# Gate and up products of both feed-forwards by Strassen's seven quarter products, the down products in a phase of their own

## The chip, the cores and the metric

The kernel runs on one core of one Trainium2 chip. The metric is the device time of one execution in microseconds (us). TensorE (PE) does the matrix products, VectorE (DVE), ScalarE (ACT) and GpSimd (POOL) the elementwise work, and every transfer between the chip's memory (DRAM) and SBUF is issued by SyncE's queue (SP). Each engine takes its own instructions in their written order.

## The reference

A network of two blocks over 1024 tokens with 1024 features. The first block holds two feed-forwards with a mixer between them:

```python
def swiglu(h, w_gu, w_down):
    g, u = jnp.split(h @ w_gu, 2, axis=-1)
    return (jax.nn.silu(g) * u) @ w_down
...
mod = (cs @ w_ada[l] + b_ada[l]).reshape(B, N_MOD, D)[:, :, None, :]
sh1, sc1, gt1, sh2, sc2, gt2, sh3, sc3, gt3 = [mod[:, i] for i in range(N_MOD)]
h = modulate(rms_norm(x, g_ffn1[l]), sh1, sc1)
x = x + HALF_STEP * gt1 * swiglu(h, w_gu1[l], w_down1[l])
h = modulate(rms_norm(x, g_mix[l]), sh2, sc2)
x = x + gt2 * hybrid_mixer(h, w_in[l], gate_bias[l], g_q[l], g_k[l], g_mh[l], w_out[l])
h = modulate(rms_norm(x, g_ffn2[l]), sh3, sc3)
x = x + HALF_STEP * gt3 * swiglu(h, w_gu2[l], w_down2[l])
```

`w_gu` is 1024 x 5632 (gate columns, then up columns), `w_down` 2816 x 1024. The mixer and the second block (two layers of attention, convolution and Fourier mixing) stand outside the change. Everything is float32.

## The kernel before

The program holds activations with the features on partitions: `H[k][h]` is feature block k (128 rows, k = 0..7) of token half h (512 columns). A float32 product is done as three products of rounded parts: each operand is split into a high part, rounded by ACT, and a low part, the remainder by DVE (`split`), and `gemm` issues high·high, high·low and low·high for each k, three matmuls of 128x128 by 128x512 (L311, L312, L313).

The 2816 hidden features of a feed-forward are 22 blocks of 128. `ffn` runs `gu(f, h)` for each block f and half h: 8 k x 3 matmuls for gate, as many for up, then `swiglu`: silu on ACT (L245), the product with up on DVE (L536), the split of the result (L250 on ACT, L272 on DVE) into the pair `act[f, h]`. A whole block is 96 matmuls. The blocks stand in groups of three (the last of four). After the first block of group g the down products of group g - 1 are issued, `out(g - 1, m, h)` for 8 output blocks m and both halves, each adding its result to the resident `X[m]` on DVE (L555). `Weights` loads each slab of weights and splits it ahead of its use.

Beside each block `fill(f)` starts one `ada` chunk, a piece of the modulation vector for later stages: four loads of 512 KB (`adaw`), eight multiply-adds into `adacc` on DVE (L437, L439), four transposes of `adacc` on PE (L452) and a sum on DVE (L454). `norm_mod` makes the second half of H (L490, L478) while the first blocks already run on half 0.

All tiles come from rotating pools: "u" with 43 tiles of 128x1024 (X, H, weights, act pairs, adaw), "hf" with 14 of 128x512 (e, adacc, sums), and eight PSUM banks (`ps`). A new tile waits for the last user of the buffer it takes. On SP each transfer also waits for the transfer eight earlier.

Of the kernel before, what the change touches and what calls it, by code (L numbers as in the profile page):

```python
# [18 lines left out]
P = 128  # L19
T = 1024  # L20
HT = 512
NK = 8
# [28 lines left out]
class Pipe:  # L51
    """Software pipeline over generators: each step moves every live one on to its next yield, oldest first.
    Streams set aside start their items beside whatever else is started."""
# [22 lines left out]

    def flush(self):
# [52 lines left out]
class Stream:  # L130
    """Items that are started at a rate."""
# [25 lines left out]
class Weights:  # L157
    """Slabs of weights, loaded and split ahead of their use."""

    def __init__(self, b, views, dve=False):  # L160
        self.b, self.views, self.dve = b, views, dve
        self.stg, self.w = [], []

    def fetch(self, n):
        while len(self.stg) < min(n, len(self.views)):
            self.stg.append(self.b.fetch_w(*self.views[len(self.stg)]))
# [12 lines left out]
    def get(self, i, ahead=1):  # L179
        """Slab i; the next ones are split, ahead of them, and the two behind these on their way."""  # L180
        self.split(i + 1)
        if ahead:
            self.fetch(i + 3 + ahead)
            self.split(i + 1 + ahead)
        return self.w[i]


class Build:
# [17 lines left out]
    # storage  # L206
# [4 lines left out]
    def pair(self, name="pair"):  # L211
        """High and low parts of a [128, 512] operand."""
# [14 lines left out]
    # activation tables  # L227
# [24 lines left out]
    def recip(self, out, in_):  # L252
        """out = 1 / in_ for in_ > 0."""
# [8 lines left out]
    def rsqrt(self, out, in_, scale, eps_col):  # L262
        """out = (in_ * scale + eps) ** -0.5"""
# [14 lines left out]
    def load(self, dst, src):  # L278
        """dst on chip <- src in DRAM (float32, rounded already where dst is float32r)."""
        self.nc.sync.dma_start(dst.bitcast(F32) if dst.dtype == F32R else dst, src)  # L280

    def store(self, dst, src):
        """dst in DRAM (float32) <- src on chip (float32 or rounded float32r)."""
        self.nc.sync.dma_start(dst, src.bitcast(F32) if src.dtype == F32R else src)

    # weights and products

    def fetch_w(self, view, kk, cc):
        s = self.U(F32, (P, kk, cc), "stg")
        self.load(s, view)  # L290
        return s
# [7 lines left out]
    def cols(self, w, starts):  # L299
        """Weights of the 128-column slabs of w (rows on partitions) that begin at starts."""  # L300
# [3 lines left out]
    def gemm(self, ps, w, col, H, h, parts=1, ks=None):  # L304
        """ps += W[:, col block].T @ H[:, half h]; w = (hi, lo) slabs, H[k][h] = (hi | lo) pairs. In parts."""
# [53 lines left out]
    def load_x(self, h):  # L359
        """Half h of X from tokens to features on partitions, and each token's 1 / rms on every partition."""  # L360
# [24 lines left out]
    def ada_start(self, w, c, bias, out, c0):  # L385
        """The same as ada, on the tensor engine."""
# [16 lines left out]
    def norm_start(self, X, r, a, s, H):  # L403
        """H[:][0] in two parts, each as soon as its modulation is there."""
# [14 lines left out]
    def ada(self, w, c, bias, out, c0, row=None, ahead=False):  # L419
        """out[:, c0/128 ...] = (c @ w)[c0 : c0 + 512] + bias, features on partitions;  # L420
        or 1 + that to DRAM, row = (where, bias)."""
# [10 lines left out]
        for q in range(4):  # L432
# [7 lines left out]
            if q % 2 and not ahead:  # L440
                yield
# [15 lines left out]
    # norms  # L457

    def add_sq(self, acc, x, first):
        """acc += x * x, for [128, 512] blocks."""  # L460
# [7 lines left out]
    def total(self, acc):  # L468
        """Sums over the partitions, on every partition."""
# [4 lines left out]
    def modulate(self, t, s, H, k, h):  # L474
        """H[k][h] = hi | lo of t + s."""
# [4 lines left out]
    def norm_mod(self, X, a, s, H, h, acc, r=None):  # L480
        """H[:][h] = X / rms(X) * a + s, acc = sums of squares or r = 1 / rms; a pipeline item."""
# [14 lines left out]
    # feed-forward  # L496

    def ffn(self, H, X, wgu, wdown, gate, fill, done, late, squares=True, begin=False):
# [5 lines left out]
        act, order, views = {}, {}, []  # L504

# [4 lines left out]
        def use_down(g):  # L510
            n = len(groups[g])
            for i in range(4):
                use(("down", g, i), wdown[i][:, groups[g][0]:groups[g][0] + n], n, 256)

        for g, grp in enumerate(groups):
            for f in grp:
                for o in range(2):
                    use((f, o), wgu[o * NFF + f], NK, P)
                if f == grp[0] and g:
                    use_down(g - 1)  # L520
        use_down(G - 1)
        ws = Weights(self, views)

# [8 lines left out]

        def swiglu(f, h, pg, pu):
# [4 lines left out]
            act[f, h] = p = self.pair("act")  # L538
            self.split(e, p[:, 0], p[:, 1])
# [8 lines left out]

        def out(g, m, h, acc=None):
            A = [[act[f, 0], act[f, 1]] for f in groups[g]]  # L550
            ps = self.ps()
            yield from self.gemm(ps, ws.get(order["down", g, m // 2]), (m % 2) * P, A, h)
# [11 lines left out]
        n = 2  # L564
        if begin:
            n = 3
# [10 lines left out]
        pipe.until(self.whole(H, 1))  # L577
        for f in range(n):
            pipe.go(gu(f, 1, 1 if f == n - 1 else 0))
        for f in range(n):  # L580
            fill(f)
# [1433 lines left out]
```

## Time and profile before

| | |
|---|---|
| time, median of 3 runs | 3357.47 us (3354.01 to 3358.36) |
| span of the profiled execution | 3352.6 us |
| PE busy | 3265.7 us, 97% |
| DVE, ACT, POOL busy | 59%, 38%, 6% |
| first feed-forward | about 33 to 760 us |
| second feed-forward | about 1490 to 2225 us |
| memory traffic | 368 MB, 110 GB/s over the span |

The profiled execution's own time is not listed apart from its span; the median of the runs lies 4.9 us above the span. PE's busy share is that of pipelined matmuls whose ends are modelled: the page gives one 128x512 matmul some 391 ns, while the next starts well before that, so what a matmul costs is read from the distance of starts in the timeline.

### The profile page before, as it was taken

How to read it: one execution, taken by the hardware profiler on the slowest of the kernel's cores; microseconds unless marked ns; L12 is line 12 of the kernel's file. 1: busy time of each engine (PE TensorE's matmuls, PEld its weight loads, DVE VectorE, ACT ScalarE, POOL GpSimd, SP SyncE). 2: the span in 40 equal slices, each digit the busy share in tenths (PEclk: the TensorE clock that was granted, in tenths of full speed). 3: DMA queues.
4: the chain of work that ended last, by engine and by line, in shares of the span. 5: the costliest groups of instructions: out<-in, count | busy, mean ns of one | idle time of the engine just before them, and what ended most of it. 6: DMA issues, size and time to landing. Idle time of an engine off the chain costs nothing.

```text
span 3352.6 us, 38177 instructions
## 1 busy us (share of the span) xinstructions
PE 3265.7 (97%) x14876; PEld 2673.0 (80%) x14876; DVE 1964.5 (59%) x2981; ACT 1263.3 (38%) x2063; POOL 198.2 (6%) x144
## 2 busy tenths in 40 slices
PE   8999999999999979999999999989999999999999
PEld 5888888887877768888888888878888777878877
DVE  7644543336378877666454332264746886565786
ACT  4111111124366554552111111244445834444770
POOL 0000000000122242410000000000000000000000
PEclk9999999999999979999999999999999999999999
DMA  5433321113444456453333211123421233332232
GB/s 209 151 121 113 118 90 52 55 57 113 147 139 134 120 166 183 123 196 120 113 114 110 63 48 47 60 88 118 121 81 58 89 138 127 119 111 64 73 135 107
DMA packets 131172, 368.05 MB, mean 110 GB/s; under 512 B 14872, under 2 KB 16792, under 8 KB 130992
## 3 DMA queue, kind: packets, MB, share of 16 engines
q1 hardware_dynamic: 130992, 365.62, 34.3%
q8 instruction: 117, 1.92, 0.2%
q14 instruction: 63, 0.52, 0.0%
HBM read 294.05 MB, written 71.51 MB: 109 GB/s over the span
## 4 chain that ended last, share of the span: by engine, by line
PE 87%; DVE 5%; ACT 4%; issue 2%; DMA 1%; POOL 0%; SPq 0%; DVEq 0%; ACTq 0%; POOLq 0%
PE ps L311 22%; PE ps L313 22%; PE ps L312 22%; PE ps L1431 2%; PE ps L1432 2%; PE ps L1433 2%; PE ps L1638 2%; PE ps L1714 1%; PE ps L1715 1%; PE ps L1713 1%; PE ps L1699 1%; PE ps L1700 1%; PE ps L619 1%; ACT bE L245 1%; DVE mS L276 1%
## 5 line engine op out<-in xcount | busy, mean ns | idle before, releaser
L311 PE MATMUL ps<-H,wh 128*128 128x512 f32 x2512 | 990.1, 394 | 15.9 <-ACT wh L250 12.1
L313 PE MATMUL ps<-H,wl 128*128 128x512 f32 x2512 | 982.8, 391 | 1.2 <-DVE wl L272 1.1
L312 PE MATMUL ps<-H,wh 128*128 128x512 f32 x2512 | 981.2, 391 | 0.0
L311 PEld LDWEIGHTS ps<-H,wh 128*128 128x128 f32 x2512 | 473.5, 189 | 119.2 <-ACT wh L250 13.3
L313 PEld LDWEIGHTS ps<-H,wl 128*128 128x128 f32 x2512 | 473.5, 189 | 103.3 <-DVE wl L272 3.0
L312 PEld LDWEIGHTS ps<-H,wh 128*128 128x128 f32 x2512 | 473.9, 189 | 98.8 <-issue 2.6
L272 DVE TENSOR_TENSOR wl<-stg,wh 128x1024 fp32r<-128x1024 f32 (+1 forms) x249 | 302.8, 1220 | 130.2 <-ACT wh L250 98.6
L250 ACT ACTIVATE wh<-stg 128x1024 fp32r<-128x1024 f32 (+1 forms) x233 | 232.4, 1009 | 310.5 <-PE ps L313 217.4
L536 DVE TENSOR_TENSOR e<-e,ps 128x512 f32<-128x512 f32 x88 | 60.5, 687 | 489.4 <-PE ps L313 489.3
L311 PE MATMUL ps<-act,wh 128*128 128x512 f32 x704 | 275.3, 391 | 0.0
L313 PE MATMUL ps<-act,wl 128*128 128x512 f32 x704 | 274.0, 389 | 0.0
L312 PE MATMUL ps<-act,wh 128*128 128x512 f32 x704 | 273.9, 389 | 0.0
L555 DVE SCALAR_TENSOR_TENSOR x<-ps,coef,x 128x512 f32<-128x512 f32 x224 | 167.5, 749 | 147.4 <-PE ps L313 147.3
L250 ACT ACTIVATE act<-e 128x512 fp32r<-128x512 f32 x88 | 55.6, 632 | 449.7 <-DVE e L536 443.3
L1641 DVE TENSOR_REDUCE bmc<-ps 128x1 f32<-128x512 f32 x256 | 164.6, 683 | 49.9 <-PE ps L1638 49.9
L245 ACT ACTIVATE e<-ps 128x512 f32<-128x512 f32 x88 | 52.5, 597 | 347.9 <-PE ps L313 347.9
L245 ACT ACTIVATE bE<-ps 128x512 f32<-128x512 f32 x256 | 138.2, 590 | 103.0 <-PE ps L1700 72.8
L276 DVE TENSOR_TENSOR bEl<-bE,bEh 128x1024 fp32r<-128x1024 f32 x128 | 155.2, 1218 | 33.4 <-ACT bEh L250 17.8
L313 PEld LDWEIGHTS ps<-act,wl 128*128 128x128 f32 x704 | 132.1, 188 | 27.6
L312 PEld LDWEIGHTS ps<-act,wh 128*128 128x128 f32 x704 | 132.2, 188 | 27.4 <-issue 0.2
L311 PEld LDWEIGHTS ps<-act,wh 128*128 128x128 f32 x704 | 132.2, 188 | 27.3 <-issue 0.2
L250 ACT ACTIVATE bEh<-bE 128x1024 fp32r<-128x1024 f32 x128 | 135.5, 1058 | 22.7 <-DVE wl L272 9.3
(332 smaller groups left out, 4897.0 us busy)
## 6 DMA issues: line engine op xcount, KB each, us to landing
adaw<-in_w_ada SPq DMA_DIRECT2D x120, 512.0 KB, 5.8
stg<-in_w_gu SPq DMA_DIRECT2D x88, 512.0 KB, 3.6
stg<-in_w_in SPq DMA_DIRECT2D x69, 512.0 KB, 5.0
stg<-in_w_down SPq DMA_DIRECT2D x48, 384.0 KB, 4.3
stg<-in_w_out SPq DMA_DIRECT2D x28, 512.0 KB, 7.5
y<-y SPq DMA_DIRECT2D x22, 512.0 KB, 6.7
q<-qk SPq DMA_DIRECT2D x32, 256.0 KB, 3.5
bQ<-q SPq DMA_DIRECT2D x16, 512.0 KB
```

Of the source, the lines that this page charges most:

```text
L245: i = self.nc.scalar.activation(out, in_, func, **kw)
L250: self.nc.scalar.activation(out, in_, AF.Copy, scale=scale)
L272: self.nc.vector.tensor_tensor(lo, src, hi.bitcast(F32), OP.subtract)
L276: eng.tensor_tensor(lo, e, hi.bitcast(F32), OP.subtract)
L311: mm(ps, wh, rh, start=k == 0, stop=False)
L312: mm(ps, wh, rl, start=False, stop=False)
L313: mm(ps, wl, rh, start=False, stop=k == n - 1)
L555: nc.vector.scalar_tensor_tensor(x, ps, gate[:, m:m + 1], x, OP.mult, OP.add)
L1431: mm(o, y[:, 0, ts], wh[:, j], start=i == j == 0, stop=False)
L1432: mm(o, y[:, 0, ts], wl[:, j], start=False, stop=False)
L1433: mm(o, y[:, 1, ts], wh[:, j], start=False, stop=i == 3 and j == 1)
L1641: nc.vector.tensor_reduce(mc[:, 8 * h + i:8 * h + i + 1], pss[h], AX.X, OP.max)
```

## The change

Of the 22 blocks of each feed-forward the first three keep their classical products (`n = 3`). For the other 19, gate and up are taken together as a 2x2 product of quarters: A is the weights of block f (gate, up by the lower and upper four k), B is H (lower and upper four k by the two token halves), and Strassen's method in Winograd's form makes it with seven quarter products of 4 k x 3 = 12 matmuls. The sums of B's quarters (`combine`: 16 additions of high and low parts on DVE, 16 sums on POOL, 16 splits) are made once for each feed-forward, beside the three classical blocks; the sums of the weights' quarters (`sums`, four for each block, on POOL) and the splits of the seven left operands (`prep`) run four products ahead. Results come together in three PSUM banks x, y, z; three copies to SBUF on ACT and three additions on DVE for each block (`products`). The activations of blocks 0 to 17 go to DRAM (`spill`) and come back (`fetch_act`); X goes to DRAM too and is loaded again. All down products run behind the last block, the last group as before. An `ada` chunk is now started every 14 products in the first eight cases, the others in the down phase.

```diff
-            if q % 2 and not ahead:
+            if not ahead:
                 yield
...
+    def combine(self, H, B):
...
+        for k in range(4):
+            x = {}
+            for n, i, h in (("11", k, 0), ("12", k, 1), ("22", 4 + k, 1), ("21", 4 + k, 0)):
+                x[n] = self.half(name="hs")
+                p = H[i][h].bitcast(F32)
+                v(x[n], p[:, 0], p[:, 1], OP.add)
...
+                nc.gpsimd.tensor_tensor(t[n], a, b, op)
+            yield
+            for n in ("t2", "t1", "t3", "t4"):
+                B[n][k] = p = self.pair("T")
+                self.split(t[n], p[:, 0], p[:, 1])
...
+    SEVEN = (("a11", "b11", "x"), ("a12", "b21", "y"), ("s2", "t2", "x"), ("s1", "t1", "z"), ("s3", "t3", "x"),
+             ("s4", "b22", "z"), ("a22", "t4", "x"))
+
+    SUMS = {-1: ("s1", "a21", "a22", OP.add), 0: ("s2", "s1", "a11", OP.subtract),
+            2: ("s3", "a11", "a21", OP.subtract), 3: ("s4", "a12", "s2", OP.subtract)}
+    LAG = 4
...
+                    Wr[i, name] = t = self.half(name="ws")
+                    nc.gpsimd.tensor_tensor(t, Wr[i, a], Wr[i, b], op)
...
+                self.split(Wr[i, self.SEVEN[j][0]], p[:, 0], p[:, 1])
+                if j == 2:
+                    fetch(i + 2)
...
+        for n, (i, j) in enumerate(seq):
+            beside(n)
+            prep(n + self.LAG)
...
+            w, b, s = W.pop(n), B[self.SEVEN[j][1]], self.SEVEN[j][2]
+            o = acc[s]
+            for k in range(4):
+                wh, wl = (w[:, q, k * P:(k + 1) * P] for q in range(2))
+                mm(o, wh, b[k][:, 0], start=k == 0 and s not in started, stop=False, skip_group_check=True)
+                mm(o, wh, b[k][:, 1], start=False, stop=False, skip_group_check=True)
+                mm(o, wl, b[k][:, 0], start=False, stop=k == 3, skip_group_check=True)
+            started.add(s)
+            if j in (0, 2, 3):
+                c = self.half(name="pc")
+                self.copy(c, o)
+                held[j] = c
+            elif j == 6:
+                g.send(o)
+                pipe.start(g)
+            else:
+                c = self.half(name="pq")
+                nc.vector.tensor_tensor(c, o, held[{1: 0, 4: 3, 5: 2}[j]], OP.add)
+                g.send(c)
...
-        groups = [range(f, f + 3) for f in range(0, 18, 3)] + [range(18, 22)]
+        n, kept = 3, range(18, NFF)
+        groups = [[18, 19, 20]] + [list(range(f, f + 3)) for f in range(0, 15, 3)] + [[15, 16, 17, 21]]
...
+            nc.vector.tensor_tensor(g0, g0, u0, OP.mult)
+            nc.vector.tensor_tensor(g1, g1, u1, OP.mult)
...
+            if f in kept:
+                act[f, h] = p
+            else:
+                self.store(AD[f, h].rearrange("s p n -> p s n"), p)
...
+            if i % 14 == 3 and i < 105:
+                fill()
...
+        for g in range(G - 1):
+            for m in range(NK):
+                for h in range(2):
+                    pipe.go(out(g, m, h))
+                if g == 0:
+                    load_x(m + 2)
+                if m in (1, 5) and g:
+                    fill()
+                if m in (2, 4):
+                    fetch_act(g + 1, (m - 2) // 2)
...
+            self.store(XD[m * P:(m + 1) * P, HALVES[h]], x)
...
+        for k in range(NK):
+            self.store(XD[k * P:(k + 1) * P], X[k])
```

The last two pieces put X into DRAM: half by half in `w_out` ahead of the second feed-forward, whole at the start ahead of the first.

PE at the end of a block beside which a chunk of the modulation is made (first feed-forward). Before, the four transposes of `adacc` stand between two `gu` halves:

```order
L313 MATMUL ps_1395<-H_518,wl_1291 128x512
L452 MATMUL ps_1459<-ident_63,adacc_1371 128x128 [waits DVE_49]
L452 MATMUL ps_1459<-ident_63,adacc_1371 128x128 x3
L311 MATMUL ps_1469<-H_587,wh_1260 128x512
L312 MATMUL ps_1469<-H_587,wh_1260 128x512
```

Now they stand between the seventh product of one block (bank `ps_1597`, the last operand `T_930`) and the first product of the next:

```order
L601 MATMUL ps_1597<-T_930,W_1642 128x512
L602 MATMUL ps_1597<-T_930,W_1642 128x512
L603 MATMUL ps_1597<-T_930,W_1642 128x512
L469 MATMUL ps_1753<-ident_63,adacc_1659 128x128 [waits DVE_49]
L469 MATMUL ps_1753<-ident_63,adacc_1659 128x128 x3
L601 MATMUL ps_1765<-H_265,W_1666 128x512 [waits PE_49]
```

The transposes have moved from behind a half of a classical block to the seam between two blocks of seven products.

DVE at the same two places, up to the last multiply-add into `adacc`, for which the transposes wait. Before:

```order
L439 SCALAR_TENSOR_TENSOR adacc_1371<-adaw_1386,cs_87,adacc_1371 128x512 [waits DVE_49]
L272 TENSOR_TENSOR wl_1399<-stg_1254,wh_1398 128x1024 [waits DMAHW4_49,Activation_49]
L439 SCALAR_TENSOR_TENSOR adacc_1371<-adaw_1390,cs_87,adacc_1371 128x512 [waits DMAHW1_49,DVE_49]
L272 TENSOR_TENSOR wl_1429<-stg_1288,wh_1428 128x1024 [waits DMAHW5_49,PE_49,Activation_49]
L439 SCALAR_TENSOR_TENSOR adacc_1371<-adaw_1390,cs_87,adacc_1371 128x512 [waits DVE_49]
L536 TENSOR_TENSOR e_1383<-e_1383,ps_1322 128x512 [waits PE_49]
```

Now, where L614 is the addition that follows the sixth product (j = 5) and L685 the multiplication with `g1`, whose silu needs that addition:

```order
L614 TENSOR_TENSOR pq_1702<-ps_1597,pc_1681 128x512 [waits PE_49,Activation_49]
L277 TENSOR_TENSOR W_1738<-ws_1640,W_1738 128x512 [waits Activation_49]
L277 TENSOR_TENSOR W_1762<-ws_1708,W_1762 128x512 [waits Activation_49]
L614 TENSOR_TENSOR pq_1729<-ps_1599,pc_1657 128x512 [waits PE_49]
L456 SCALAR_TENSOR_TENSOR adacc_1659<-adaw_1732,cs_87,adacc_1659 128x512 [waits DMAHW3_49]
L685 TENSOR_TENSOR pq_1729<-pq_1729,pq_1702 128x512 [waits Activation_49]
L456 SCALAR_TENSOR_TENSOR adacc_1659<-adaw_1732,cs_87,adacc_1659 128x512 [waits DVE_49]
L684 TENSOR_TENSOR pq_1633<-pq_1633,ps_1597 128x512 [waits PE_49]
```

Before, the last multiply-add stood ahead of the DVE instructions that wait for PE; now it stands behind two that do, the addition L614 and, through silu, L685. In the first chunk of each feed-forward it stands behind L684 as well, which waits for the seventh product.

SP where the classical blocks end in the first feed-forward. Before, the chunks' loads stand there:

```order
L280 DMA adaw_830<-in_w_ada 128x1024 [waits DMAHW7_49,PE_49]
L280 DMA adaw_834<-in_w_ada 128x1024 [waits DMAHW0_49,DVE_49,PE_49]
L280 DMA adaw_839<-in_w_ada 128x1024 [waits DMAHW1_49,PE_49]
L280 DMA adaw_843<-in_w_ada 128x1024 [waits DMAHW5_49,DMAHW2_49,DVE_49]
L280 DMA adaw_853<-in_w_ada 128x1024 [waits DMAHW7_49,DMAHW3_49,DVE_49]
```

Now the stores of X and of activations stand there, and behind them the weights of the first blocks that go by seven products:

```order
L289 DMA xspill_128<-x_102 128x1024 [waits DMAHW1_49,DVE_49]
L289 DMA act_220<-act_581 128x2x512 [waits DMAHW2_49,DVE_49]
L289 DMA act_220<-act_637 128x2x512 [waits DMAHW3_49,DVE_49]
L289 DMA act_220<-act_659 128x2x512 [waits DMAHW4_49,DVE_49]
L289 DMA act_220<-act_732 128x2x512 [waits DMAHW5_49,DVE_49]
L289 DMA act_220<-act_853 128x2x512 [waits DMAHW6_49,DVE_49]
L285 DMA stg_939<-in_w_gu1 128x1024 [waits DMAHW7_49,PE_49]
```

The load of `stg_939`, the first weights of block 3, is issued only when DVE has finished the pair `act_853`, the second half of block 1.

## Rows read from the trace of the kernel before

**Rows 1.** The page's part 1: busy us, share of the span, instructions.

```profile
PE 3265.7 (97%) x14876; PEld 2673.0 (80%) x14876; DVE 1964.5 (59%) x2981; ACT 1263.3 (38%) x2063; POOL 198.2 (6%) x144
```

**Rows 2.** Stretches: length, busy PE, PEld, DVE, ACT, POOL, granted clock, DMA share, GB/s.

```profile
120.00:300.00 180.00, 180.00 (x810) 149.20 (x809) 92.77 (x132) 29.42 (x39) 0.00 (x0) 1.00 0.38 121
...
1500.00:1700.00 200.00, 200.00 (x888) 164.66 (x887) 110.97 (x156) 42.73 (x59) 0.00 (x0) 1.00 0.35 112
```

**Rows 3.** What PE waited for, 33 to 760 us: total, times, longest.

```profile
PE ps L311 <- ACT wh L250: 4.2, 1, 4.2
...
PE ps L313 <- DVE wl L272: 0.8, 1, 0.8
PE ps L452 <- DVE x L376: 0.2, 1, 0.2
```

**Rows 4.** PE's timeline in a classical block: start, duration; eleven matmuls, first and last.

```profile
77.69 0.39 PE L312 MATMUL ps<-H,wh 128*128 128x512 f32 x1
...
79.96 0.39 PE L313 MATMUL ps<-H,wl 128*128 128x512 f32 x1
```

**Rows 5.** DVE by line and shape, 33 to 760 us: busy us, mean ns, idle before.

```profile
L439 DVE SCALAR_TENSOR_TENSOR adacc<-adaw,cs,adacc 128x512 f32<-128x512 f32 x112 | 83.3, 750 | 9.3 <-DMA adaw<-in_w_ada 7.1
L555 DVE SCALAR_TENSOR_TENSOR x<-ps,coef,x 128x512 f32<-128x512 f32 x106 | 79.4, 749 | 69.7 <-PE ps L313 69.7
...
L272 DVE TENSOR_TENSOR act<-e,act 128x512 fp32r<-128x512 f32 x44 | 30.4, 692 | 23.1 <-ACT act L250 22.4
L536 DVE TENSOR_TENSOR e<-e,ps 128x512 f32<-128x512 f32 x44 | 30.2, 687 | 232.6 <-PE ps L313 232.5
L272 DVE TENSOR_TENSOR wl<-stg,wh 128x768 fp32r<-128x768 f32 x24 | 22.9, 956 | 8.5 <-ACT wh L250 3.3 <-issue 2.5 <-PE ps L312 2.1
```

**Rows 6.** ACT by line and shape, whole span.

```profile
L250 ACT ACTIVATE act<-e 128x512 fp32r<-128x512 f32 x88 | 55.6, 632 | 449.7 <-DVE e L536 443.3 <-issue 4.9 <-DVE wl L272 1.5
L245 ACT ACTIVATE e<-ps 128x512 f32<-128x512 f32 x88 | 52.5, 597 | 347.9 <-PE ps L313 347.9
```

**Rows 7.** POOL by line and shape, whole span (an mLSTM stage of the mixer).

```profile
L836 POOL TENSOR_TENSOR mE<-mE 128x512 f32<-128x512 f32 x32 | 47.2, 1476 | 99.0 <-DVE mE L828 52.2 <-DVE mS L276 34.8 <-PE ps L843 8.1
```

**Rows 8.** DVE by line and shape, beside POOL in the mixer and elsewhere.

```profile
L272 DVE TENSOR_TENSOR wl<-stg,wh 128x1024 fp32r<-128x1024 f32 x201 | 257.0, 1284 | 114.0 <-ACT wh L250 92.7 <-PE ps L312 16.7 <-PE ps L1714 1.0
...
L276 DVE TENSOR_TENSOR mS<-mE,mS 128x512 fp32r<-128x512 f32 x48 | 37.7, 797 | 2.0 <-ACT mS L250 1.5
```

**Rows 9.** Timeline of POOL and of DVE in the mixer around 982 us.

```profile
981.66 1.02 POOL L836 TENSOR_TENSOR mE<-mE 128x384 f32<-128x384 f32 x1 [8.27 <-issue]
...
982.09 1.67 DVE L272 TENSOR_TENSOR wl<-stg,wh 128x1024 fp32r<-128x1024 f32 x1
```

**Rows 10.** Timeline of PE around 62 us: start, duration, idle before.

```profile
62.56 1.47 PE L311 MATMUL ps<-H,wh 128*128 128x512 f32 x4 [1.90 <-ACT H L413]
```

**Rows 11.** Stretches behind that idle time; columns as in rows 2.

```profile
64.00:66.00 2.00, 2.00 (x7) 1.54 (x6) 2.00 (x5) 0.62 (x1) 0.00 (x0) 0.50 0.00 0
66.00:68.00 2.00, 2.00 (x9) 1.63 (x8) 0.80 (x4) 0.00 (x0) 0.00 (x0) 0.82 0.03 8
```

**Rows 12.** DVE's timeline beside the second halves of blocks 0 to 2.

```profile
84.73 0.69 DVE L272 TENSOR_TENSOR act<-e,act 128x512 fp32r<-128x512 f32 x1
92.69 0.69 DVE L536 TENSOR_TENSOR e<-e,ps 128x512 f32<-128x512 f32 x1 [7.28 <-PE ps L313]
...
114.66 0.68 DVE L536 TENSOR_TENSOR e<-e,ps 128x512 f32<-128x512 f32 x1
```

**Rows 13.** A stretch at the start, when only transfers set the pace; columns as in rows 2.

```profile
34.00:38.00 4.00, 3.24 (x8) 2.06 (x7) 4.00 (x7) 2.44 (x3) 0.00 (x0) 0.50 1.03 410
```

**Rows 14.** The page's part 6, transfers: KB each, median us from issue to landing.

```profile
adaw<-in_w_ada SPq DMA_DIRECT2D x120, 512.0 KB, 5.8
stg<-in_w_gu SPq DMA_DIRECT2D x88, 512.0 KB, 3.6
```

**Rows 15.** DVE's timeline where the second feed-forward opens.

```profile
1502.89 0.75 DVE L490 SCALAR_TENSOR_TENSOR nrm<-x,coef,rstd 128x512 f32<-128x512 f32 x1 [4.31 <-ACT rstd L245]
```

More of the change, by code (lines that the diff above doesn't have):

```diff
@@ L75, in go, with beside @@
                 f.feed(self)
+    def beside(self):
+        for f in self.side:
+            f.feed(self)
     def flush(self):
@@ L290, in fetch_w, with fetch_rows @@
         self.load(s, view)
+        return s
+    def fetch_rows(self, w, blocks):
+        s = self.U(F32, (P, len(blocks), w.shape[2]), "stg")
+        at = 0
+        while at < len(blocks):
+            n = 1
+            while at + n < len(blocks) and blocks[at + n] == blocks[at] + n:
+                n += 1
+            self.load(s[:, at:at + n], w[:, blocks[at]:blocks[at] + n])
+            at += n
         return s
@@ L508, in use @@
             views.append(view)
[L510 to L521, printed above, removed]
+        for f in range(n):
+            for o in range(2):
+                use((f, o), wgu[o * NFF + f], NK, P)
         ws = Weights(self, views)
+        wd = Weights(self, [(i, grp) for grp in groups for i in range(4)])
+        wd.load = lambda i, grp: self.fetch_rows(wdown[i], grp)
         def gu(f, h, ahead=2, parts=1):
@@ L547, in gu_start, with post, fetch_act @@
             yield from swiglu(f, 0, *p)
+        def post(f):
+            g0 = yield
+            self.act(g0, g0, AF.Silu)
+            u1 = yield
+            g1 = yield
+            self.act(g1, g1, AF.Silu)
+            u0 = yield
+            yield
+            yield
+            nc.vector.tensor_tensor(g0, g0, u0, OP.mult)
+            nc.vector.tensor_tensor(g1, g1, u1, OP.mult)
+            yield
+            spill(f, 0, g0)
+            yield
+            spill(f, 1, g1)
+        def fetch_act(g, h):
+            for f in groups[g]:
+                if f not in kept:
+                    act[f, h] = p = self.pair("act")
+                    self.load(p, AD[f, h].rearrange("s p n -> p s n"))
         def out(g, m, h, acc=None):
@@ L551, in out @@
             ps = self.ps()
[L552 removed]
+            yield from self.gemm(ps, wd.get(4 * g + m // 2), (m % 2) * P, A, h)
             yield
@@ L577, in ffn, with beside, load_x @@
         pipe.until(self.whole(H, 1))
+        B = {}
+        sums = self.combine(H, B)
         for f in range(n):
-            pipe.go(gu(f, 1, 1 if f == n - 1 else 0))
-        for f in range(n):
-            fill(f)
-        for g, grp in enumerate(groups):
-            for f in grp:
-                if f >= n:
-                    for h in range(2):
-                        pipe.go(gu(f, h))
-                    fill(f)
-                if f == grp[0] and g:
-                    for m in range(NK):
-                        for h in range(2):
-                            pipe.go(out(g - 1, m, h))
+            pipe.go(gu(f, 1, 1 if f == n - 1 else 0, 4), 8)
+            if f == 0:
+                pipe.start(sums)
+        pipe.until(lambda: (id(H), "combined") in self.ready)
+        rest = list(range(n, NFF))
+        def beside(i):
+            if i % 14 == 3 and i < 105:
+                fill()
+            if i == 7 * len(rest) - 4:
+                wd.fetch(1)
+            if i == 7 * len(rest) - 1:
+                wd.split(1)
+        self.products(rest, lambda f, o: (wgu[o * NFF + f], NK, P), B, post, beside)
+        def load_x(k):
+            if k < NK:
+                X[k] = self.U(name="x")
+                self.load(X[k], XD[k * P:(k + 1) * P])
+        load_x(0)
+        load_x(1)
+        for g in range(G - 1):
[8 more added lines that the diff above has]
+                    fetch_act(g + 1, (m - 2) // 2)
         pipe.step()
```

76 lines of the change are left out of this document (61 added, 15 removed).

## The prediction

> **What bounds the kernel now.** I read the page's busy shares first: PE is busy 97% of the span, DVE 59%, POOL 6% [rows 1]. Then windows over the two feed-forwards: in stretches of 180 and 200 us PE is busy for the whole of it, at the full granted clock (1.00, the 2.4 GHz level), while DVE is busy 93 of 180 and 111 of 200 us and the DMA engines 35 to 38% [rows 2]. Then PE's own waits: from 33 to 760 us the longest is 4.2 us, which is at the start, the others shown are under 1 us, and the transposes of the modulation chunks wait 0.2 us in all [rows 3]. So in a feed-forward nothing but the number of matmuls sets the time, and a matmul that goes away is worth its distance to the next. That distance is in the timeline: eleven matmuls start between 77.69 and 79.96 us, ten distances, 0.227 us each [rows 4]; the 0.39 us of a row is the pipelined length and is not what one costs.
>
> **What the change removes.** A block of 96 matmuls becomes seven products of 12, 84; 12 x 19 blocks x 2 feed-forwards = 456 matmuls. The down products keep their number. 456 x 0.227 = 103.4 us.
>
> **What it adds in the steady state.** For each block of seven products: DVE makes seven low parts of operands and two of activations (0.69 us each by the act row), three additions and two multiplications (0.69): 14 x 0.69 = 9.7 us. A chunk of the modulation is eight multiply-adds of 0.75 and a sum, about 6.4 us, every second block, 3.2 a block. Together 12.9 us [rows 5] of the 84 x 0.227 = 19.0 us that PE takes. ACT: nine roundings of 0.63, three copies of bank results and two silus of 0.60: 8.7 us [rows 6]. POOL: four sums of 128x512; the nearest row is the same operation and shape in the mixer, 1.48 us [rows 7], 5.9 us. Loads are 1 MB, stores 1 MB and half a chunk 1 MB a block: 3 MB in 19 us, 160 GB/s, where the start of the kernel moves 410 [rows 13]. All fit under PE. What must be in time: a bank is read out while one product on another bank runs, 12 x 0.227 = 2.72 us, by a copy of 0.60 or an addition of 0.69; operands are split four products ahead, 10.9 us. So I cost the steady state at nothing while DVE's queue is not held up by more than 1.8 us just before the addition behind the fifth product, the one after which PE needs the same bank (x) one product later.
>
> **DVE beside POOL.** POOL was idle in both feed-forwards [rows 2] and now works beside DVE. In the mixer, where it does, a DVE subtraction of 128x512 with both inputs in SBUF takes 0.80 us on the mean [rows 8] against 0.69 in the feed-forward [rows 5], and one of 128x1024 that began during a POOL operation took 1.67 [rows 9] against a mean of 1.28 [rows 8]. So there is some hindrance, by 0.11 us on the mean. Nine such operations a block would add 1 us to 12.9: absorbed. If instead each POOL operation kept DVE out for all its length, two blocks with one chunk would need 2 x 9.7 + 6.4 + 8 x 1.48 = 37.6 us of DVE in PE's 38.1: still inside, with no room. I take 2 us in all for what lies badly, 0 to 15 (0.4 us a block) as bounds.
> The Trainium skill speaks against the change here: its page "SBUF — State Buffer", section "Who interferes with whom", says that a DVE instruction with two SBUF inputs and a GpSimd instruction that reads SBUF exclude each other for the whole instruction. By that rule the 2 us would go to the upper end of 15, and rival 2 below becomes likelier; the trace agrees that the two hinder each other, but its mean of 0.80 us is far from a full exclusion at every meeting.
>
> **The modulation chunks.** In the order now, the last multiply-add of a chunk stands behind the addition that follows the sixth product, and behind the multiplication that needs silu of it. From the end of that product: 0.69 addition, 0.60 silu beside a multiply-add of 0.75, 0.69 multiplication, 0.75 multiply-add, some 0.3 for the handovers: 3.2 us, and PE reaches the transposes after one product, 2.72 us. It waits 0.5 us, 14 times. In the first chunk of each feed-forward it stands behind the multiplication that waits for the seventh product too: 0.69 + 0.75 + 0.2 = 1.6 us, twice. Before, PE never waited there [rows 3]. Also the chunk's last load is issued when the fourth product ends, 5.4 us before the sixth does, and a load of that kind lands after 5.8 us, a lighter one after 3.6 [rows 14]: mostly hidden, at worst 1 us more each. Sum 7 + 3.2 = 10 us; bounds 0, if the chain is quicker than its rows, and 25, with late loads.
>
> **The way into the products.** In the first feed-forward DVE is through with H at 85.4 us, and the second halves of blocks 0 to 2 end at about 92.5 and 114.5 [rows 12]. Between these stands the chain of `combine`: four additions on DVE, 2.8 us, to 88.2; 16 sums on POOL at 1.48, 23.6 us, to 111.8; rounding and low part of the last, 1.3 us, to 113.1; then the low part of the first left operand, 113.8. PE needs it at 114.5 + 0.5. A margin of 1.2 us in a chain of 25 is none: DVE must also do the classical blocks' activations between, and SP issues the first weights only behind the store of block 1's second half. I take 2 us, bounds 0 and 8 (the chain longer by the 15% of 0.80 to 0.69 is 3.8, and PE's clock as below). In the second feed-forward H is there about 10 us earlier against its blocks: 0.
> The opening of the second feed-forward also has its weights' loads behind the stores of X, and there DVE waits 4.3 us for the norm as it is [rows 15]: 1.5 us, 0 to 4.
>
> **The down phase.** A group is 144 matmuls, 32.6 us. DVE: 16 multiply-adds of 0.75, four low parts of 0.96, two chunks of 6.4: 28.6 us at most [rows 5], and only in groups with two chunks. Transfers there are 3 MB of activations, 1.5 of weights and 4 of chunks, 8.5 MB or 260 GB/s of 410 [rows 13]. The first weights and X are loaded some 16 us ahead. Stores and reloads of activations and X thus cost nothing while loads land within that, against 3.6 to 5.8 us [rows 14]. For the two seams between the phases 2 us, 0 to 10.
>
> **Sum.** 103.4 - (2 + 10 + 2 + 1.5 + 2) = 85.9 us off. The profiled span of 3352.6 us becomes 3266.7; the median of the runs stands 4.9 above the span, so 3271.6, **3272 us**. With every cost at its lower bound 3254; with every one at its upper, 62 us, 3316.
>
> **Rivals.**
> 1. *The stalls do not show* (chance 0.17): DVE's chains are shorter because starts overlap the ends of the instructions before. Then 3254 to 3262. For it: PE hardly waits in the present feed-forwards. Against it: the chunk's chain, which is new.
> 2. *DVE's queue sets the pace* (0.16): POOL's operations keep DVE out for their whole length, or the chunk loads come late and hold back everything behind them on DVE. With 37.6 of 38.1 us taken, a slip of 1 us per block is not made up: 38 x 1 = 38 us, and with 1.6 us 61: 3290 to 3335. For it: the 1.67 us of [rows 9]. Against it: the mean of 0.80.
> 3. *Slower than before* (0.06): the addition behind the fifth product comes late in every block, so that PE stands idle before the seventh, and then runs at a lower clock. After 1.90 us without work [rows 10] the trace shows the clock at 0.50 (the 1.2 GHz level) for 2 us and 0.82 in the next 2 [rows 11]: about 1.4 us of work lost on top. A late addition by 1.8 (its margin) plus 1.9 us, in every block, is 1.9 + 1.4 = 3.3 us against a gain of 12 x 0.227 = 2.72 a block: 38 x 0.6 = 23 us slower, 3380 (and with the other costs up to 3400). It decides from 2.72 us a block, an addition about 3.1 us later than it could be. For it: the queue in order, with waits for loads in it. Against it: DVE is 32% idle, and only every second block has a chunk.
> 4. *It does not do what it says*: the matmuls are counted in the order of both programs, so the removal is sure; the chance of a balance within 0.2% (6.7 us) is 0.02, a point between 2 and 3.
>
> **How the numbers follow.** The likeliest case, 3262 to 3288, has 0.59. Rival 1 has 0.17, rival 2 0.16, rival 3 0.06, even 0.02. The range is 3254 to 3316: the main case, nearly all of rival 1 and half of rival 2, about 0.82. A measurement of this kernel tells 0.2% from no change. Faster by more: 0.92; within: 0.02; slower: 0.06.
>
> **What the profile after would show.** PE's busy time less by about 103 us; in the stretches of seven products 44 matmuls per 10 us but for short gaps. Gaps before the transposes of chunks, named after the multiply-add on DVE, near 0.5 us, 16 times, the first of each feed-forward longer. PE before the first quarter product of the first feed-forward: a wait of a few us on a low part. DVE's subtractions near 0.8 us in the products where they were 0.69; POOL's sums near 1.5. No wait on ACT's copies and none on loads in the down phase. I am wrong if PE waits on DVE's additions in every block (rival 3), if DVE's busy time in the products comes near 100% (rival 2), if the granted clock falls there, or if the distance of matmuls within a product is more than 0.227 us.

## The result and the profile after

The changed kernel takes 3316.74 us (median of 4 runs, 3313.98 to 3317.88) against 3356.95 before on the same chip: a ratio of 0.9882, 95% interval 0.9868 to 0.9896. It is faster by 40 us where 85 were forecast, and lies just above the range. Rival 2, DVE's queue sets the pace, had named 3290 to 3335. Each run below stands beside runs of the kernel before, whose medians lie between 3354.3 and 3357.0 us, so a difference of two or three us between runs says nothing.

The page's part 1 after the change:

```profile
span 3312.2 us, 38901 instructions
...
PE 3180.8 (96%) x14420; PEld 2594.4 (78%) x14420; DVE 2218.0 (67%) x3349; ACT 1413.6 (43%) x2399; POOL 486.8 (15%) x328
```

Against [rows 1] PE is busy 84.9 us less, not 103.4: 18.5 us of the matmuls that went away came back as matmuls that take longer. And PE's idle time, span less busy, went from 86.9 to 131.4 us, 44.5 more. 84.9 - 44.5 = 40.4 us, the difference of the spans. So 63 us of the 103.4 are to be found: 44.5 in waits, 18.5 in matmuls that took longer; the mean granted clock fell from 0.989 to 0.985, by estimate at most 0.004 x 3181 = 13 us of these (the mean counts idle time too). The two feed-forwards share it: the mixer's first sum on POOL begins 17.3 us earlier than before (883.3 for 900.6), the first transposes behind the second feed-forward 40.3 us earlier (2181.8 for 2222.1), where each was to give some 43.

What PE waited for in the first feed-forward (total, times, longest), the answer to [rows 3]:

```profile
PE ps L469 <- DVE adacc L456: 13.9, 8, 5.4
PE ps L601 <- ACT W L255: 8.9, 1, 8.9
...
PE ps L601 <- DVE pq L614: 1.6, 1, 1.6
```

And in the second, 1480 to 2180 us:

```profile
PE ps L469 <- DVE adacc L456: 11.2, 6, 3.8
PE ps L601 <- DVE pq L614: 3.1, 1, 3.1
PE ps L488 <- DVE adacc L456: 2.8, 2, 1.5
PE ps L601 <- ACT W L255: 1.8, 1, 1.8
```

The lines to see are L469 and L488, PE waiting for the multiply-adds of a modulation chunk: 27.9 us, 16 times, where 10 were forecast. The other great piece is one single wait of 8.9 us, before the first quarter product of the first feed-forward. (The waits of 5.4 and 3.8 us are those of the first chunk of each feed-forward, while DVE was still catching up from the opening.) The granted clock around it (stretches of 4 us; PE busy first, the clock is third from the end):

```profile
116.00:120.00 4.00, 0.00 (x0) 0.00 (x0) 4.00 (x3) 3.25 (x7) 4.00 (x3) 0.68 0.48 146
120.00:124.00 4.00, 1.05 (x2) 0.50 (x2) 4.00 (x7) 1.78 (x3) 0.07 (x1) 0.50 0.99 344
124.00:128.00 4.00, 3.29 (x8) 2.48 (x8) 1.43 (x3) 0.06 (x1) 3.65 (x3) 0.50 1.03 415
128.00:132.00 4.00, 4.00 (x12) 3.10 (x11) 3.39 (x3) 3.33 (x6) 4.00 (x3) 0.61 0.36 147
```

After 8.9 us without work PE runs at 0.50 (the 1.2 GHz level) until about 131 us. DVE is busy nearly all the time in which PE waits, from 114.1 to 122.95 us; it stands idle once, for 0.7 us. DVE and POOL there, in the timeline (start, duration, operations in a row):

```profile
85.06 4.91 DVE L527 TENSOR_TENSOR hs<-H 128x512 f32<-128x512 f32 x8
...
102.55 9.28 DVE L277 TENSOR_TENSOR T<-ht,T 128x512 fp32r<-128x512 f32 x8
...
117.19 7.03 DVE L277 TENSOR_TENSOR T<-ht,T 128x512 fp32r<-128x512 f32 x8
```

```profile
87.11 4.01 POOL L533 TENSOR_TENSOR ht<-hs 128x512 f32<-128x512 f32 x1 [86.67 <-DVE hs L527]
91.19 1.29 POOL L533 TENSOR_TENSOR ht<-ht,hs 128x512 f32<-128x512 f32 x1
...
118.36 1.71 POOL L533 TENSOR_TENSOR ht<-hs,ht 128x512 f32<-128x512 f32 x1
```

Eight low parts on DVE took 9.28 us, 1.16 each, where eight additions of the same size in a row had taken 4.91, 0.61 each. The first POOL sum took 4.01 us, the next 1.29: DVE had its eight additions in a row from 85.06 to 89.97, and the sum ended 1.15 us behind them. DVE in turn then stood idle for 5.0 us, until POOL had read the buffers that its next additions (L527) were to take. The last sum of `combine` ended at 120.1 us where the forecast had 111.8.

Two chains led to PE's start and ended within 2 us of each other. DVE finished the pair `act_853` only at 117.27 us; behind its store SP issued the first weights' load (117.75), and ACT's rounding of these weights released PE's first matmul at 122.95. The third matmul needs the low part of the same weights, which stands in DVE's queue behind the last low parts of T (the split operands that `combine` makes): it was ready at 124.83 us, and that matmul started at 124.88.

In the steady state, 160 to 540 us, DVE's operations by line and shape (busy us, mean ns, idle before):

```profile
L277 DVE TENSOR_TENSOR W<-ws,W 128x512 fp32r<-128x512 f32 x68 | 52.9, 798 | 31.0 <-ACT W L255 31.0
L277 DVE TENSOR_TENSOR W<-stg,W 128x512 fp32r<-128x512 f32 x49 | 41.1, 863 | 4.4 <-ACT W L255 4.3
L456 DVE SCALAR_TENSOR_TENSOR adacc<-adaw,cs,adacc 128x512 f32<-128x512 f32 x49 | 39.7, 811 | 1.0
L614 DVE TENSOR_TENSOR pq<-ps,pc 128x512 f32<-128x512 f32 x54 | 37.2, 689 | 69.3 <-PE ps L603 69.2
```

Operations with both inputs in SBUF are stretched, the low parts to 0.80 and 0.86 us for 0.69 and the multiply-add to 0.81 for 0.75; the addition L614, one of whose inputs is PSUM, takes 0.689. Means hide where this falls. One chunk close by, DVE and then POOL:

```profile
230.19 0.68 DVE L614 TENSOR_TENSOR pq<-ps,pc 128x512 f32<-128x512 f32 x1
230.79 2.38 DVE L277 TENSOR_TENSOR W<-ws,W 128x512 fp32r<-128x512 f32 x2
233.09 0.68 DVE L614 TENSOR_TENSOR pq<-ps,pc 128x512 f32<-128x512 f32 x1
233.69 1.18 DVE L456 SCALAR_TENSOR_TENSOR adacc<-adaw,cs,adacc 128x512 f32<-128x512 f32 x1
234.79 0.68 DVE L685 TENSOR_TENSOR pq<-pq 128x512 f32<-128x512 f32 x1
235.39 0.74 DVE L456 SCALAR_TENSOR_TENSOR adacc<-adaw,cs,adacc 128x512 f32<-128x512 f32 x1
```

```profile
231.00 1.62 POOL L574 TENSOR_TENSOR ws<-ws,stg 128x512 f32<-128x512 f32 x1 [10.23 <-issue]
232.58 1.74 POOL L574 TENSOR_TENSOR ws<-stg 128x512 f32<-128x512 f32 x1
```

While POOL works, from 231.00 to 234.3, two low parts take 2.38 us and a multiply-add 1.18. The addition L614 of 0.68 us at 233.09, beside POOL as well, is not stretched. It starts late, and with it the chain of the chunk behind it, by about a microsecond. PE waited 1.44 us at this seam.

### The profile page after: what moved, and what is told of

Read it like the earlier page. It is cut to its first block, busy times and chain, and to the rows that moved or that the text cites. A ratio compares the mean times of both kernels' runs of the same rounds, so it can differ in the third digit from the quotient of the medians.

```text
span 3312.2 us, 38901 instructions
## 1 busy us (share of the span) xinstructions
PE 3180.8 (96%) x14420; PEld 2594.4 (78%) x14420; DVE 2218.0 (67%) x3349; ACT 1413.6 (43%) x2399; POOL 486.8 (15%) x328
## 4 chain that ended last, share of the span: by engine, by line
PE 46%; DVE 5%; ACT 2%; issue 2%; DMA 2%; POOL 0%; SPq 0%; DVEq 0%; ACTq 0%; POOLq 0%
PE ps L328 8%; PE ps L330 8%; PE ps L329 8%; PE ps L601 2%; PE ps L603 2%; PE ps L602 2%; PE ps L1806 2%; PE ps L1882 2%; PE ps L1883 1%; PE ps L1599 1%; PE ps L1867 1%; PE ps L1600 1%; PE ps L1601 1%; PE ps L1881 1%; PE ps L1868 1%
## 5 line engine op out<-in xcount | busy, mean ns | idle before, releaser
L328 PE MATMUL ps<-H,wh 128*128 128x512 f32 x1296 | 515.7, 398 | 16.6 <-ACT wh L255 12.5
L330 PE MATMUL ps<-H,wl 128*128 128x512 f32 x1296 | 510.2, 394 | 1.9 <-DVE wl L277 1.9
L329 PE MATMUL ps<-H,wh 128*128 128x512 f32 x1296 | 508.5, 393 | 0.0
L328 PEld LDWEIGHTS ps<-H,wh 128*128 128x128 f32 x1296 | 245.9, 190 | 72.4 <-ACT wh L255 14.2
L330 PEld LDWEIGHTS ps<-H,wl 128*128 128x128 f32 x1296 | 245.7, 190 | 56.7 <-DVE wl L277 3.9
L329 PEld LDWEIGHTS ps<-H,wh 128*128 128x128 f32 x1296 | 246.2, 190 | 51.1 <-issue 1.7
L255 ACT ACTIVATE wh<-stg 128x1024 fp32r<-128x1024 f32 (+1 forms) x157 | 154.0, 990 | 308.8 <-PE ps L329 96.4
L277 DVE TENSOR_TENSOR wl<-stg,wh 128x1024 fp32r<-128x1024 f32 (+1 forms) x173 | 210.0, 1220 | 75.7 <-ACT wh L255 68.7
L601 PE MATMUL ps<-T,W 128*128 128x512 f32 x608 | 237.6, 391 | 5.5 <-DVE pq L614 4.8
L602 PE MATMUL ps<-T,W 128*128 128x512 f32 x608 | 237.3, 390 | 0.0
L603 PE MATMUL ps<-T,W 128*128 128x512 f32 x608 | 237.1, 390 | 0.0
L601 PE MATMUL ps<-H,W 128*128 128x512 f32 x456 | 182.6, 400 | 10.7 <-ACT W L255 10.7
L603 PE MATMUL ps<-H,W 128*128 128x512 f32 x456 | 179.8, 394 | 1.4 <-DVE W L277 1.4
L602 PE MATMUL ps<-H,W 128*128 128x512 f32 x456 | 179.8, 394 | 0.0
L614 DVE TENSOR_TENSOR pq<-ps,pc 128x512 f32<-128x512 f32 x114 | 78.5, 688 | 137.8 <-PE ps L603 137.6
```

Of the source, the lines that this page charges most:

```text
L255: self.nc.scalar.activation(out, in_, AF.Copy, scale=scale)
L277: self.nc.vector.tensor_tensor(lo, src, hi.bitcast(F32), OP.subtract)
L328: mm(ps, wh, rh, start=k == 0, stop=False)
L329: mm(ps, wh, rl, start=False, stop=False)
L330: mm(ps, wl, rh, start=False, stop=k == n - 1)
L601: mm(o, wh, b[k][:, 0], start=k == 0 and s not in started, stop=False, skip_group_check=True)
```

## The experiments

Theory A: a POOL sum and a DVE operation with two SBUF inputs keep each other out for their whole length; this makes `combine` and the chunks' chain late. Rival B: it is the order of the queues alone, the first weights' load behind a store on SP and the last multiply-add behind waiting instructions on DVE. Ratios are to the kernel before, with the 95% interval behind them; the changed kernel's is 0.9882.

**Without POOL's sums.** The operands take plain quarters.

```diff
...
-                nc.gpsimd.tensor_tensor(t[n], a, b, op)
...
-                    Wr[i, name] = t = self.half(name="ws")
-                    nc.gpsimd.tensor_tensor(t, Wr[i, a], Wr[i, b], op)
+                    Wr[i, name] = Wr[i, a]
```

> Leaves out all sums that GpSimd made (the combine sums and the weights' sums): the seven left and the T operands take a plain quarter in their place, so the result is not the reference's; every other instruction stays. Theory A (a GpSimd sum and a VectorE operation with two SBUF inputs keep each other out for their whole length): the wait before the first quarter product (8.9 us in the first feed-forward) falls under 2 us, the waits before the chunks' transposes fall from 1.2 to 1.4 us to about 0.5, VectorE's low parts in the products go from 0.80-0.86 to 0.69 us; about 30 us faster than the changed kernel, 3283 to 3292. Rival B (the order of the queues alone: the first weights' load behind a store, the last multiply-add behind two waiting instructions): chunk waits stay at 1.2 us or more, the first wait stays at 5 us or more, 3303 to 3315.

It took 3267.1 us, ratio 0.9737 [0.9723, 0.9752], 50 us faster than the changed kernel and more than either theory expected. Of the waits that the change brought into the first feed-forward one is left; the eight low parts take 4.90 us for 9.28, and the mean from 160 to 540 us is 0.69 again:

```profile
PE ps L469 <- DVE adacc L456: 2.7, 1, 2.7
```

```profile
93.88 4.90 DVE L277 TENSOR_TENSOR T<-hs,T 128x512 fp32r<-128x512 f32 x8
...
104.76 4.90 DVE L277 TENSOR_TENSOR T<-hs,T 128x512 fp32r<-128x512 f32 x8
```

This takes two things away at once: POOL's work beside DVE, and the time in which somebody waits for a sum. The next two runs part them.

**Sums that nobody reads.** POOL makes all its sums, at the same places; the operands are plain quarters as above.

```diff
...
-                    Wr[i, name] = t = self.half(name="ws")
-                    nc.gpsimd.tensor_tensor(t, Wr[i, a], Wr[i, b], op)
+                    Wr[i, name] = Wr[i, a]
+                    t0 = self.half(name="ws")
+                    nc.gpsimd.tensor_tensor(t0, Wr[i, a], Wr[i, b], op)
```

> GpSimd makes every sum at its old place, but nobody reads them: the operands take plain quarters, as in the run without sums (so the result is not the reference's). This takes the lateness of the sums out of the chain and leaves GpSimd's work beside VectorE. If the two engines keeping each other out is the cause: chunk waits back above 1 us each, low parts in the products again 0.80 us or more, 3295 to 3316. If it was that operands had to wait for sums that GpSimd makes slowly: 3267 to 3273, as without sums.

It took 3330.8 us, 0.9927 [0.9911, 0.9944], more than either alternative had: all of the 50 us are lost again, and 14 more. No operand waits for a sum here, so it is the making of the sums that costs. What still waits for POOL is DVE, for buffers that POOL reads in `combine`, in the first feed-forward:

```profile
DVE hs L527 <- POOL ht L534: 6.2, 2, 5.1
```

From 160 to 540 us DVE waits for POOL nowhere, and its operations are long all the same:

```profile
L277 DVE TENSOR_TENSOR W<-stg,W 128x512 fp32r<-128x512 f32 x117 | 95.0, 832 | 25.4 <-ACT W L255 25.3
...
L687 DVE TENSOR_TENSOR pq<-pq 128x512 f32<-128x512 f32 x18 | 22.8, 1269 | 8.0 <-ACT pq L250 7.7
```

PE waited 18.2 and 15.3 us before transposes in the two feed-forwards: now POOL's sums fall on the multiplication with `g1` (1.27 us for 0.75), which stands in the chunk's chain, and DVE is busy 2248.9 us over the span, 31 more than with the sums that are read. That this makes the 14 us more is read from these lines, and no run tested it.

**Memsets in the sums' place.** Three for each unread sum, into the same buffer and about as long on POOL, but they only write.

```diff
...
+                    for _ in range(3):
+                        nc.gpsimd.memset(t0, 0.0)
```

> The same, with three GpSimd memsets of 128x512 (0.53 us each in the kernel before, 1.6 us in all) in the place of each unread sum: as long on GpSimd, but they only write. Also not the reference's result. If it is reading from SBUF that keeps the two apart: VectorE's low parts at 0.69 us, 3266 to 3273. If any GpSimd work beside VectorE does it: as the run with unread sums, 3295 to 3316.

It took 3264.2 us, 0.9727 [0.9712, 0.9741]: as without POOL's work, though POOL is as busy as with sums (478 us for 487). POOL over the span, and DVE from 160 to 540 us:

```profile
L578 POOL MEMSET ws<- 128x512 f32 x456 | 234.1, 530 | 445.4 <-DVE act L277 336.7 <-DVE pq L618 84.4 <-issue 7.8
```

```profile
L277 DVE TENSOR_TENSOR W<-stg,W 128x512 fp32r<-128x512 f32 x112 | 74.7, 686 | 27.2 <-ACT W L255 26.3
...
L454 DVE TENSOR_SCALAR adacc<-adaw,cs 128x512 f32<-128x512 f32 x9 | 5.1, 568 | 10.0 <-DMA adaw<-in_w_ada 10.0
```

So it is not POOL's being busy, but its reading from SBUF beside DVE operations with two SBUF inputs. This is what the Trainium skill states ("SBUF — State Buffer", "Who interferes with whom"): a DVE instruction with two SBUF inputs contends with a GpSimd instruction that reads SBUF, not with one that only writes it. The runs agree on both halves, 0.83 against 0.69 us. The memsets do lengthen one other operation of DVE, the first multiplication of a chunk (L454, one tensor in SBUF and a scalar): 0.57 us on the mean for 0.49 with the sums. They also free DVE of the 6.2 us for buffers in `combine`; what those cost alone no run tests.

**All sums on DVE.**

```diff
-                nc.gpsimd.tensor_tensor(t[n], a, b, op)
+                nc.vector.tensor_tensor(t[n], a, b, op)
...
-                    nc.gpsimd.tensor_tensor(t, Wr[i, a], Wr[i, b], op)
+                    nc.vector.tensor_tensor(t, Wr[i, a], Wr[i, b], op)
```

> All these sums on VectorE in place of GpSimd. Theory A: VectorE does 16 + 16 + 16 + 6 operations of 0.61 us for combine and the classical blocks, 33 us from 85 us, so the low part for the first quarter product is ready near 120 in place of 124.8 us; chunk waits near 0.5 us; 3288 to 3302. Rival B: VectorE has 16 sums more in its queue and 2.4 us more a block, nothing is gained, the chunk waits grow: 3317 to 3335.

It took 3285.25 us, 0.9797 [0.9782, 0.9811]: 31 us faster than the changed kernel, a little below the expected band, although DVE has 184 operations more. Over the whole span DVE is busy 2218.0 us in the changed kernel; without the sums, and with all of them on DVE, part 1 of the pages has:

```profile
PE 3170.4 (97%) x14420; PEld 2589.1 (79%) x14420; DVE 2143.8 (66%) x3349; ACT 1413.8 (43%) x2399; POOL 198.2 (6%) x144
```

```profile
PE 3172.9 (97%) x14420; PEld 2590.7 (79%) x14420; DVE 2253.5 (69%) x3533; ACT 1416.6 (43%) x2399; POOL 198.6 (6%) x144
```

POOL's sums thus lengthened DVE's work by 74 us in all, and making them itself costs DVE 110. So POOL's sums did relieve DVE in total; the time was lost by where the lengthening fell. PE's waits in the first feed-forward, with the sums on DVE:

```profile
PE ps L469 <- DVE adacc L456: 7.3, 8, 1.3
PE ps L601 <- ACT W L255: 2.2, 1, 2.2
PE ps L603 <- DVE W L277: 1.2, 1, 1.2
```

The 8.9 us fell to 2.2 + 1.2; the chunk waits to 0.9 each, which is the order's part together with the sums that now stand in DVE's queue.

**Only `combine`'s sums on DVE; only the weights' sums on DVE.** The first or the second half of the edit above.

> Only the 16 sums of combine on VectorE, the weights' sums stay on GpSimd. Theory A: the opening of the products shortens (the first product's wait of 8.9 us to 3 or less, with the half clock behind it), the chunk waits after the opening stay at 1.2 to 1.4 us: 3298 to 3306. If the opening were not a matter of GpSimd's exclusion but of the load behind a store: 3312 or more.

> Only the weights' sums on VectorE, combine stays on GpSimd. Theory A: the opening's 8.9 us stays, but the chunk waits fall to about 1 us and the 1.6 and 5.4 us behind the opening fall; 3300 to 3308, and the gains of this run and of the one with combine alone add up to about that of both (31 us). If only the opening matters: 3314 or more.

The first took 3314.15 us, 0.9873 [0.9858, 0.9888], the second 3293.7 us, 0.9815 [0.9800, 0.9830]. The second is 6 us better than its band; the first missed: `combine` alone on DVE gains 2.6 us, within the runs' spread. PE's opening waits in the first of the two, in the first feed-forward and then in the second:

```profile
PE ps L603 <- DVE W L277: 4.9, 1, 4.9
PE ps L601 <- ACT W L255: 2.1, 1, 2.1
```

```profile
PE ps L603 <- DVE W L277: 6.3, 1, 6.3
```

With `combine` done by DVE earlier, the weights' sums on POOL start at 114.17 us and fall on the last low parts of T and the first of W; the wait moves from the rounding to the low part, 7.1 us for 9.6. In the second feed-forward the opening became longer, 2.0 + 6.3 us for 1.8 + 0.6. The contention went where both engines have work next, so the gains of 2.6 and 23 us do not add up to the 31 of both, as the expectation had it. The first run's time lies in the band that was named for the load behind a store; but the wait that is left ends with DVE's low part, not with the load.

**First weights loaded ahead of the stores.** The first two blocks' loads are issued behind the second half of block 0.

```diff
         fetch(0)
         fetch(1)
+        yield
...
+            if f == 0:
+                pipe.start(sums)
+                next(prods)
```

> The weights of the first two blocks that go by seven products are loaded right behind the first classical block's second half, ahead of the stores of activations that VectorE makes late. Theory A: VectorE's queue, not the load, sets the first quarter product; its wait of 8.9 + 0.7 us moves from the rounding on ScalarE to the low part on VectorE and stays above 7 us; 3311 to 3317. Rival B: the wait falls under 3 us in the first feed-forward, with the half clock behind it: 3301 to 3307.

It took 3319.05 us, 0.9898 [0.9881, 0.9914], so nothing was gained, and the time lies 2 us above theory A's band. PE's waits in the first feed-forward, then DVE's last low parts of T and POOL's sums beside them:

```profile
PE ps L604 <- DVE W L277: 8.8, 1, 8.8
PE ps L602 <- ACT W L255: 7.2, 1, 7.2
```

```profile
116.69 13.45 DVE L277 TENSOR_TENSOR T<-ht,T 128x512 fp32r<-128x512 f32 x8
```

```profile
119.53 1.72 POOL L574 TENSOR_TENSOR ws<-stg 128x512 f32<-128x512 f32 x1
121.33 1.59 POOL L574 TENSOR_TENSOR ws<-ws,stg 128x512 f32<-128x512 f32 x1
122.88 1.71 POOL L574 TENSOR_TENSOR ws<-stg 128x512 f32<-128x512 f32 x1
```

The load was early, the weights' sums began early, at 119.53 us for 124.27, right behind those of `combine`, and the eight low parts now took 13.45 us, 1.68 each, in turn with the sums. Rival B's first half did not come: with the load early, DVE's queue holds the product back. But this edit also moved POOL's sums onto DVE's low parts, so it does not price the load alone; the last run below does.

**Transposes one step later.**

```diff
+        if not ahead:
+            yield
         ps = self.ps([P, 4, P])
         for j in range(4):
             nc.tensor.transpose(ps[:, j], acc[:, j * P:(j + 1) * P], self.ident)
```

> Only the transposes of a modulation chunk are issued one step (one quarter product or down product) later. Both theories: the 25 us of waits before transposes in all fall under 4 us, and the half clock after the first one (5.4 us) goes; the rest stays. 3288 to 3296. If instead what VectorE finishes late then holds up the banks, the waits reappear as waits of the first matmul of a product on an addition, and the time stays at 3310 or more.

It took 3289.3 us, 0.9805 [0.9791, 0.9820]: 27 us faster than the changed kernel, as expected. Of the waits before transposes 1.0 and 2.7 us are left in the two feed-forwards; the opening of the first stays:

```profile
PE ps L603 <- ACT W L255: 8.9, 1, 8.9
PE ps L603 <- DVE pq L616: 2.4, 1, 2.4
```

So the seam is where the delay became PE's: a late DVE costs nothing as long as PE has a product to do.

**Both mends, without and with the early loads.**

> All sums on VectorE and the chunks' transposes one step later, both together. In the run with the sums on VectorE alone PE still waited 7.3 and 7.5 us before transposes in the two feed-forwards and 2.4 us before the chunk rows; if the two causes are separate, these go and nothing else comes: 3268 to 3273, near the forecast for the change itself. If VectorE with the sums in its queue is too slow for the additions, the waits reappear at the first matmul of a product: 3278 or more.

> As the version with all sums on VectorE and late transposes, with the first two blocks' weights loaded ahead of the stores as well. The wait before the first product was 2.2 + 1.2 us and 1.4 + 1.3 us with sums on VectorE: if the load sets it, 2 to 5 us faster than without (3264 to 3270); if VectorE's queue sets it, the same (within 2 us).

They took 3266.4 us, 0.9736 [0.9722, 0.9751], and 3267.7 us, 0.9740 [0.9724, 0.9756]. The first is the best version that computes the whole network: 50 us faster than the changed kernel, 90 faster than the kernel before. Of the waits that the change brought, these are left in its first feed-forward:

```profile
PE ps L603 <- ACT W L255: 2.1, 1, 2.1
PE ps L605 <- DVE W L277: 1.2, 1, 1.2
```

The early loads add nothing (2.1 + 0.5 us are left there), so it is DVE's queue that sets these 3.3 us too: in both versions ACT's rounding of the first weights stands behind roundings of T that wait 5.7 us for DVE's sums. Alone the two mends gain 31 and 27 us, together 50, so in part they remove the same waits: the exclusion makes DVE late, and the order of the queues decides where PE pays for it.

## Why the prediction was wrong, by its steps

- *What the change removes*: right. In the best version, which issues the same matmuls, PE is busy 3165.8 us, 99.9 less than before, and the time is 90 us below the kernel before; the run with memsets comes out 91 below. The rest of the 103.4 us are the waits and clock losses that remain.
- *What bounds, the steady state, ACT and loads*: right in their sizes. Between chunks PE runs without gaps, and behind the opening no load sets a wait in the products or the down phase; from 560 to 600 us PE is busy for the whole of the 40.
- *DVE beside POOL* is the step that failed: "I take 2 us in all for what lies badly, 0 to 15". The runs price POOL's sums at 50 us (without them) or 31 (on DVE), and the excess shows as longer waits in the next two terms. I took the hindrance from a mean in the mixer, 0.80 us [rows 8], but there the two met only now and then: of those 48 rows of 128x512, 39 took 0.67 to 0.73 us and 9 took 0.94 to 1.78. The single row of 1.67 us [rows 9] was the meeting itself. Where both engines have work without a break, a pair takes nearly the sum of its times: 1.68 us, where the low part alone takes 0.61 and the sum alone 1.29. This is close to the rule of the Trainium skill that I had cited ("SBUF — State Buffer", "Who interferes with whom"), by which the two exclude each other.
- *Rival 2*, which that rule makes likelier, had a chance of 0.16 and the right time, but only half of the mechanism. It had DVE without room in every block; from 160 to 540 us DVE is busy 231.57 of 380 us. POOL does keep DVE out, but the time went at the seams of the chunks and at the openings, so that its band held is in part luck.
- *The way into the products*: 2 us taken, bounds 0 and 8, measured 8.9 + 0.7 in the first feed-forward and 1.8 + 0.6 in the second, with 1.6 and 3.1 us behind them, and 5.4 and 3.8 (counted with the chunks) before DVE had caught up, and half clock behind the longer ones. The chain that I wrote down lets POOL's 16 sums run at their mean and leaves DVE free beside them. What was missing is that DVE's operations and these sums do not overlap, and that DVE waits for buffers that POOL still reads. Without POOL's sums, and with memsets in their place, PE waits not at all there; but these runs also take the time of the sums out of the chain, so whether its margin of 1.2 us would have held without the exclusion is not shown.
- *The modulation chunks*: the chain and its place were right, and the size was off: 10 us for 27.9. Without the exclusion 7.0 us are left in all (plain quarters) or 5.7 (memsets); the rest is the exclusion, which falls on the low parts, the multiply-add and the multiplication of that chain.
- *Rival 3*, PE idle before the seventh product at every block: did not come. That wait (L601 for L614) is seen twice, 1.6 and 3.1 us, both near the opening.
- *The clock*: only rival 3 and the bound of 8 us had a place for it; behind the single wait of 8.9 us PE ran at 0.50 for some 8 us, about 4 us of work lost on top.
- *The sum*: the 4.9 us between span and median were not one thing. The time of every later run stands 1.7 to 2.0 us above its own span, and the rest is the spread of the runs, so the forecast was some 3 us high on this account.

Open is how the 18.5 us of longer matmuls divide among the waits (in the best version 15 of them are gone along with the waits), and why the unread sums cost 14 us more than the read ones.

## What to carry to other kernels

Before work is moved to an engine that was idle, ask whether it shares something with the one that it relieves: here two thirds of what GpSimd's sums saved VectorE came back as longer operations (74 of 110 us), some of them just where TensorE was to wait for VectorE, and the kernel was 31 us slower than with the sums on VectorE. A cost per meeting is to be read from single rows where both are at work, not from the mean of a group. And a result that is due at a seam of TensorE's work is better asked for one step later: that alone gave 27 us, for two lines.

## What the runs showed of the hardware

When VectorE (two SBUF inputs) and GpSimd (reading SBUF) both have work without a break, they take turns, one operation each: low parts that take 0.61 us each in a row (4.90 us for eight) then take 1.68 each (13.45 us for eight). Which side waits longer is not fixed: eight additions of VectorE in a row kept the first GpSimd sum until their end, 4.01 us for 1.29. An operation of VectorE with one input in PSUM beside the same GpSimd work keeps its 0.689 us, and GpSimd memsets disturb neither kind; they do lengthen VectorE's multiplication of one SBUF tensor by a scalar, 0.57 us on the mean for 0.49. The mean over a stretch, 0.80 to 0.86 us, tells little of either case.
